# Moving full-precision transposes and state products together on TensorE in a hybrid encoder block

## The chip, the cores and the metric

The kernel runs on one core of a Trainium2 chip, in one launch. The metric is the device time of an execution in microseconds, taken as the median of several runs. A profile of one execution (the profiled execution) gives the trace: which engine ran which instruction when. The engines are TensorE (PE: matrix multiplies and transposes, results in PSUM), VectorE (DVE), ScalarE (ACT), GpSimd (POOL) and SyncE (SP, which issues most DMAs). Each engine works through its own queue in a fixed order; they meet through semaphores. "PE at" and "PE mm" in the profile's lines name the PSUM tile that is written (`at` or `mm`); they are no waits.

## The reference

One layer on x of 512 tokens by 1024 channels. Cut to what matters here:

```python
h = rms_norm(x, mix_norm_g)
proj = h @ w_in          # mLSTM q,k,v,o,gates | neighbourhood q,k,v | memory q | merge gates
y_ml = mlstm_branch(...) # 4 heads of 128, forward and backward, states per 64-token chunk
y_na = neighbourhood_attention(...)  # 8 heads of 64 on an 8 x 64 grid, 16 columns wide
y_xa = memory_cross_attention(...)   # 4 heads of 128 into 256 memory tokens
merged = g_ml*(y_ml @ w_br_ml) + g_na*(y_na @ w_br_na) + g_xa*(y_xa @ w_br_xa)
x = x + merged @ w_out
x = x + conv_glu_ffn(rms_norm(x), ...)   # d_ff = 2816
return rms_norm(x)
```

All of it is float32. The mLSTM branch weighs query-key products with exponentials of gate sums and adds what a running state (C) holds for the chunks before (or, backward, behind). Neighbourhood attention is softmax attention with a bias table, in windows.

## The kernel before

**Precision.** A large product is made of three fp32r matmuls: each operand is split into a high part (ScalarE copies it to fp32r) and a low part (VectorE subtracts), and `mm3` (lines 212 to 215) multiplies high by high, high by low and low by high. Small products and all transposes (against `ident`) run on TensorE in plain float32.

**Stream of weights.** The weights lie in DRAM as a list of blocks in the order of use. `weights(key)` (line 201) has SP load three blocks ahead (`wr`) and has ScalarE and VectorE split one block ahead (`wh` at line 195, `wl` at line 196). `proj(key, ...)` (line 395) then runs 24 matmuls of 512 columns (256 for the memory keys) into one PSUM tile of the pool `mmp` (four banks, tag `mm`). The small stages use the pool `atp` (four banks, tag `at`).

**Side work in steps.** The mixers are written as Python generators: `ml_all` (mLSTM), `xa_all` (memory attention), `na_all` (neighbourhood attention). They run one after another, and `step(n)` (line 1108) advances the current one by n `yield`s, with fractions kept in `quota`. The main code calls `step` inside and after its projections, so that each piece of a mixer stands between the matmuls of a projection. `drain` (line 1181) runs a mixer to its end before its branch product needs the result. Functions put on the list `late` are emitted by `flush` at certain places in `proj` and in `states`. The program text gives each instruction its rank; the order of each engine's queue is then worked out for the whole program before it runs, so an instruction may stand ahead of earlier text if its inputs are ready sooner. `tc.issue_after(ins)` keeps an instruction behind `ins` on the same engine.

**mLSTM, one head h, two steps.** `keys(h)` (line 679) transposes the head's keys with four turns (line 684), splits keys and queries, and puts on `late` the function `weigh`, which scales the values (lines 705, 709, 711). `states(h)` (line 718) multiplies keys by weighed values: four float32 products (line 729; each product is two instructions) and two `mm3` (line 732), then adds up the running states C (lines 741, 743) and splits them (line 747). `exps` makes the exponentials, `mask` adds the causal mask. `weights_J(h, o)` (line 757) does the half o of the head: two query-key products (line 765), `turn_J` for the half before (turns of the pair weights E, line 804), the edge chunk's product with C (line 769), and the *pair product* with the split states, one `mm3` of 258 columns (line 772); then VectorE forms the weights E (lines 776 to 791). `values_J` (line 808) multiplies the turned E by the values. In the loop (line 865) the first step of head h ends with `load_R(h + 1)` (two DMAs of the gate rows on SP) and `keys(h + 1)`, whose splits are kept behind `st["inter"]` and `st["mix"]`, the end of this step's pair product; the second step ends with `states(h + 1)`.

**Neighbourhood attention, 16 steps i (8 heads, two half grids).** `prep` splits queries and keys of a pair of heads, with the low parts of the queries in zero-padded tiles `QZ` (two pairs of tiles, line 906). `scores(i)` (line 934): four fp32r matmuls, then bias, exponential and normalisation on VectorE and ScalarE. `transposes(i)` (line 960): four turns (line 963) and their split into two tiles `w` (tag `E`, two buffers). `values(i)` (line 975): four fp32r matmuls (line 982). `store(i)`: lines 994 to 1003 write the split result into `yh`, `yl`. The loop (line 1011) does, in round t, scores(t), values(t - 2), transposes(t - 1). `load_vwin` has GpSimd issue 32 DMAs for the value windows of the next pair of heads, four rounds before they are needed. The rounds fall between the gate projections and branch products of the last two thirds of the merge.

Of the kernel before, what the change touches and what calls it, by code (L numbers as in the profile page):

```python
# [110 lines left out]
def hybrid_block(ctx, tc, xg, xT, memT, wflat, vecs, gbias, nabias, outa, outb, outc):  # L111
# [104 lines left out]

    def split_act(h, l, src, scale=1.0):

        A.activation(h, src, AF.Copy, scale=scale)  # L219
        V.scalar_tensor_tensor(l, src, scale, h.bitcast(F32), op0=ALU.mult, op1=ALU.subtract)  # L220


    vec = cp.tile([P, NVEC], F32, name="vec")
# [438 lines left out]
    def ml_all():  # L662
# [55 lines left out]
        def states(h, k, w, C, q, R, ee):  # L718

            flush()  # L720
            dec = ml["dec"]
            (ke, kh, kl), (ew, wh, wl) = k, w
            pc = [mmps() for _ in range(2)]
            po = (0, 130, 0, 131)
            at = lambda J, d: pc[J // 2][:, po[J] + 129 * d:po[J] + 129 * d + 129]
            for J in (0, 3, 1, 2):
                if J in (0, 3):
                    e = J // 3
                    PE.matmul(at(J, e), ke[:, e * P:(e + 1) * P], ew[e], start=True, stop=True)
                else:  # L730
                    o, js = po[J], slice((J - 1) * P, J * P)
                    mm3(pc[J // 2][:, o:o + 258], kh[:, js], kl[:, js], wh[J - 1], wl[J - 1], True, True)
            tj = [tp.tile([P, 2 * M], F32, tag="nab", name=nm("C")) for _ in range(2)]
            pair = lambda j, d: tj[j][:, 129 * d:129 * d + 129]
            one = [t[:, 258:387] for t in tj]
            C.extend([[pair(0, 0), pair(1, 0), one[0]], [one[1], pair(0, 1), pair(1, 1)]])
            for d in range(2):
                last = None
                for i in range(3) if d == 0 else range(2, -1, -1):
                    if last is None:  # L740
                        A.activation(C[d][i], at(i + d, d), AF.Copy)
                    else:
                        V.scalar_tensor_tensor(C[d][i], C[d][last], dec[:, d, i + d - 1, h:h + 1], at(i + d, d),
                                               op0=ALU.mult, op1=ALU.add)
                    last = i
            for j in range(2):
                split_act(wh[j], wl[j], tj[j][:, :258])

        def exps(h, o, R):

# [3 lines left out]
                    with tc.issue_after(st["act"]):  # L754
                        A.activation(w, w, AF.Exp, bias=ml["br"][:, d, J, h:h + 1])

        def weights_J(H, ss, h, o, k, w, C, q, R, ee):

            num = ml["num"]
            edge = 0 if o == 0 else NT - 1  # L760
            ps = {}
            for J in (o, o + 1):
                ps[J] = atps()
                hs = slice(h * S + J * P, h * S + (J + 1) * P)
                PE.matmul(ps[J][:, 384:], qT[:, hs], kT[:, hs], start=True, stop=True)  # L765
            turn_J()
            pi = {J: p[:, :258].rearrange("p (d c) -> p d c", d=2) for J, p in ps.items()}
            e, hs = 1 - edge // (NT - 1), slice(h * S + edge * P, h * S + (edge + 1) * P)
            PE.matmul(pi[edge][:, e], qT[:, hs], C[e][edge - 1 + e], start=True, stop=True)
            i = 1 if o == 0 else 2  # L770
            qs = slice((i - 1) * P, i * P)
            mm3(ps[i][:, :258], q[0][:, qs], q[1][:, qs], w[1][i - 1], w[2][i - 1], True, True)
            E = tp.tile([P, 4, P], F32, tag="E", name=nm("E"))
            y = tiny(12)
            init, den, r = [y[:, x:x + 4].rearrange("p (j d) -> p j d", j=2) for x in (0, 4, 8)]
            V.tensor_tensor(init[:, edge - o, e:e + 1], pi[edge][:, e, 128:129], num[:, e, edge, h:h + 1], op=ALU.mult)
            V.tensor_tensor(init[:, i - o], pi[i][:, :, 128], num[:, :, i, h], op=ALU.mult)
            for J in (o, o + 1):
                for d in range(2):
                    p = R[d][:, J * P:(J + 1) * P]  # L780
                    V.tensor_tensor_reduce(p, p, ps[J][:, 384:], 1.0,
                                           init[:, J - o, d:d + 1] if J == i or d == e else 0.0,
                                           ALU.mult, ALU.add, accum_out=den[:, J - o, d:d + 1])
            V.scalar_tensor_tensor(den, den, -1.0, den, op0=ALU.mult, op1=ALU.max)
            V.tensor_tensor(den, den, em.rearrange("p t (a b) -> p t a b", b=4)[:, o:o + 2, 0:9:8, h], op=ALU.max)
            V.reciprocal(den, den)
            for j in range(2):
                js = slice((o + j) * P, (o + j + 1) * P)
                V.tensor_scalar(E[:, j], R[0][:, js], den[:, j, 0:1], None, op0=ALU.mult)
                st["mix"] = V.scalar_tensor_tensor(E[:, j], R[1][:, js], den[:, j, 1:2], E[:, j], op0=ALU.mult,  # L790
                                                   op1=ALU.add).ins
            V.tensor_tensor(r, num[:, :, o:o + 2, h].rearrange("p d j -> p j d"), den, op=ALU.mult)
            Hj = lambda J: H[:, J * P:(J + 1) * P]
            A.activation(Hj(edge), pi[edge][:, e, 0:128], AF.Copy, scale=r[:, edge - o, e:e + 1])
            st["inter"] = A.activation(Hj(i), pi[i][:, 0, 0:128], AF.Copy, scale=r[:, i - o, 0:1]).ins
            V.scalar_tensor_tensor(Hj(i), pi[i][:, 1, 0:128], r[:, i - o, 1:2], Hj(i), op0=ALU.mult, op1=ALU.add)
            fresh.append((H, ss, h, o, E))
# [48 lines left out]
        last = prev = None  # L846
        open_J, turned, fresh = [], [], []

        def keyed(h, *ins):
            return keys(h, nxt, tp.tile([P, S], F32, tag="H", name=nm("ee"), bufs=4), *ins)  # L850

        def over():
            open_J.extend(fresh)
            fresh.clear()

        nxt = load_R(0)
        st_h = keyed(0)
        yield
        states(0, *st_h)
        ml["rows"]()  # L860
# [4 lines left out]
        for h in range(4):  # L865
            own, R = st_h, nxt
            values_J()
            if h > 1:
                flush()
                emit_y(h - 2, last[0])  # L870
            last = prev
            prev = tp.tile([P, S], F32, tag="H", name=nm("H"), bufs=4), tiny(4)
            weights_J(*prev, h, 0, *own)
            exps(h, 2, R)
            if h < 3:
                nxt = load_R(h + 1)
                st_h = keyed(h + 1, st["inter"], st["mix"])
                for d in range(2):
                    late.append(lambda d=d, n=nxt, i=st["mix"]: mask(n, d, i))
            over()  # L880
            yield
            values_J()
            scale = normalise(*last) if last else None
            weights_J(*prev, h, 2, *own)
            if scale:
                late.append(lambda f=scale, i=st["inter"]: f(i))
            over()
            if h < 3:
                states(h + 1, *st_h)
                exps(h + 1, 0, nxt)  # L890
            yield
        values_J()
# [10 lines left out]

    def na_all(nq, nk, vw0, yh, yl):

        QZ = [[tp.tile([P, S], F32R, tag="H", name=nm("QZ"), bufs=4) for _ in range(2)] for _ in range(2)]
        for pair in QZ:
            for e in range(2):
                G.memset(pair[e][64 - 64 * e:128 - 64 * e].bitcast(F32), 0.0)

        def prep(hp):
            qn = nq[:, hp * S:(hp + 1) * S]
            kn = nk[:, hp * S:(hp + 1) * S]
            QL = QZ[hp % 2]
            QS, KS = [], []
            for e in range(2):
                own, oth = slice(64 * e, 64 * e + 64), slice(64 - 64 * e, 128 - 64 * e)
# [42 lines left out]
        def transposes(i, sm):  # L960
# [3 lines left out]

            pp = []
            for bl in range(2):
                w = tp.tile([P, 4, P], F32R, tag="E", name=nm("w")).rearrange("p a b -> p (a b)")
                wv = w[:, :512].rearrange("p (k x q) -> p k x q", k=2, x=2)
                src = pt[:, bl * 256:(bl + 1) * 256].rearrange("p (k q) -> p k q", k=2)
                A.activation(wv[:, :, 0, :], src, AF.Copy)  # L970
                V.tensor_tensor(wv[:, :, 1, :], src, wv[:, :, 0, :].bitcast(F32), op=ALU.subtract)
                pp.append(w)
# [35 lines left out]
        sms, pts = {}, {}  # L1008
        vws = {0: vw0}
        yield  # L1010
        for t in range(n + 2):
            if t < n:
                nb = bias_tile(t + 1) if t + 1 < n else None
                sms[t] = scores(t, ops, bt)
                bt = nb
                if t % 4 == 3 and t + 1 < n:
                    ops = prep((t + 1) // 4)
            i = t - 2
            if 0 <= i:
                if i % 4 == 0 and i + 4 < n:  # L1020
                    vws[i // 4 + 1] = load_vwin(i // 4 + 1)
                store(i, values(i, pts.pop(i), vws[i // 4]))
            i = t - 1
            if 0 <= i < n:
                pts[i] = transposes(i, sms.pop(i))
            yield


# [525 lines left out]
```

## Time and profile before

| | |
|---|---|
| median of 3 runs | 873.08 us (872.96 to 873.76) |
| profiled execution | 873.18 us |
| its span, first to last instruction | 871.2 us |
| TensorE clock granted | 1.000 |
| DMA | 99.81 MB, mean 115 GB/s |

The busy share of an engine is the time in which an instruction of it was running. A line of a group gives the program line, engine, operation, written and read tiles, the count, the busy time, the mean duration in ns and the idle time before. Matmuls overlap: a 512-column matmul lasts 0.39 us in the profile, and the next one starts 0.23 us after it. In the chain that ended last, each piece is counted from the end of the piece before, so that lengths add up to the span. The profiled execution's time exceeds its span by 2.0 us.

### The profile page before, as it was taken

What the parts mean: (1) busy time and instruction counts of PE and PEld (TensorE: products, weight loads), DVE (VectorE), ACT (ScalarE), POOL (GpSimd) and SP (SyncE); (2) the same over time, 40 slices, a digit from 0 to 9 for tenths busy, and PEclk for the clock granted to TensorE, in tenths of its full rate; (3) what the DMA queues carried; (4) which work ended last, traced back from release to release, by engine and by line L of the source; (5) the groups of instructions that cost most, each with busy time, mean ns of one, the idle gap of its engine ahead of it and who ended that gap; (6) DMA issues with size and microseconds to landing.
All of it is one profiled execution on the core that took longest, in us unless ns stands there. A gap on an engine that the chain in (4) does not pass through costs nothing.

```text
span 871.2 us, 12230 instructions
## 1 busy us (share of the span) xinstructions
PE 865.8 (99%) x4287; PEld 733.9 (84%) x4287; DVE 594.7 (68%) x1292; ACT 467.8 (54%) x981; POOL 125.4 (14%) x202
## 2 busy tenths in 40 slices
PE   9999999999999999999999999999999999999997
PEld 7898889888888888888888888888888888888887
DVE  7794698997477768897676558776633466666534
ACT  7563577764355658897534455444422344444532
POOL 0101100000344370600000002111100011111010
PEclk9999999999999999999999999999999999999999
DMA  8324643533343453533223433323233323232412
GB/s 281 101 75 147 196 140 89 169 107 115 93 132 82 113 146 112 160 116 122 99 96 109 144 109 97 98 96 98 78 98 113 102 96 97 96 98 87 141 35 97
DMA packets 39421, 99.81 MB, mean 115 GB/s; under 512 B 5688, under 2 KB 13880, under 8 KB 39360
## 3 DMA queue, kind: packets, MB, share of 16 engines
q1 hardware_dynamic: 31568, 92.32, 32.6%
q0 software_dynamic: 7360, 6.32, 3.4%
q8 instruction: 34, 0.56, 0.3%
q10 hardware_dynamic: 432, 0.39, 0.1%
q14 instruction: 27, 0.22, 0.1%
HBM read 94.80 MB, written 4.21 MB: 114 GB/s over the span
## 4 chain that ended last, share of the span: by engine, by line
PE 98%; DVE 1%; issue 0%; ACT 0%; POOL 0%; POOLq 0%
PE mm L213 29%; PE mm L215 29%; PE mm L214 29%; PE at L214 2%; PE at L213 2%; PE at L215 2%; PE at L982 1%; PE at L963 1%; PE at L944 0%; PE at L945 0%; PE at L765 0%; PE at L813 0%; PE at L1070 0%; PE at L243 0%; PE mm L422 0%
## 5 line engine op out<-in xcount | busy, mean ns | idle before, releaser
L213 PE MATMUL mm<-u,wh 128*128 128x512 f32 (+1 forms) x1072 | 414.3, 386 | 0.0
L215 PE MATMUL mm<-u,wl 128*128 128x512 f32 (+1 forms) x1072 | 411.8, 384 | 0.0
L214 PE MATMUL mm<-u,wh 128*128 128x512 f32 (+1 forms) x1072 | 411.5, 384 | 0.0
L195 ACT ACTIVATE wh<-wr 128x512 fp32r<-128x512 f32 (+2 forms) x298 | 184.2, 621 | 219.9 <-PE mm L214 177.2
L196 DVE TENSOR_TENSOR wl<-wr,wh 128x512 fp32r<-128x512 f32 (+3 forms) x300 | 203.4, 681 | 88.5 <-ACT wh L195 86.4
L215 PEld LDWEIGHTS mm<-u,wl 128*128 128x128 f32 x1072 | 201.3, 188 | 40.3 <-DVE wl L196 0.4
L213 PEld LDWEIGHTS mm<-u,wh 128*128 128x128 f32 x1072 | 201.5, 188 | 39.0 <-ACT wh L195 0.4
L214 PEld LDWEIGHTS mm<-u,wh 128*128 128x128 f32 x1072 | 201.5, 188 | 38.5
L1418 POOL TENSOR_TENSOR s<-s,rb 128x512 f32<-128x512 f32 x22 | 38.2, 1736 | 401.7 <-DVE s L1417 238.9
L540 POOL DMA_DIRECT2D u<-nav_d x128 | 62.5, 535 | 70.5 <-DVE X L220 24.3
L219 ACT ACTIVATE u<-s 128x512 fp32r<-128x512 f32 x26 | 16.4, 632 | 56.4 <-DVE s L1421 56.3
L1421 DVE TENSOR_TENSOR s<-mm,s 128x512 f32<-128x512 f32 x22 | 15.2, 690 | 23.9 <-POOL s L1418 23.9
L460 ACT ACTIVATE s<-pad,vec 128x512 f32<-128x512 f32 x30 | 24.4, 813 | 9.7 <-DVE pad L458 9.7
L220 DVE SCALAR_TENSOR_TENSOR u<-s,u 128x512 fp32r<-128x512 f32 x26 | 19.1, 733 | 14.8 <-ACT u L219 14.5
L461 DVE SCALAR_TENSOR_TENSOR s<-pad,vec,s 128x512 f32<-128x512 f32 x30 | 22.5, 750 | 5.5 <-ACT s L460 5.5
L1417 DVE SCALAR_TENSOR_TENSOR s<-s,s 128x512 f32<-128x512 f32 x22 | 15.2, 691 | 13.4 <-ACT s L1416 13.3
L462 DVE SCALAR_TENSOR_TENSOR s<-pad,vec,s 128x512 f32<-128x512 f32 x30 | 22.5, 750 | 0.9
L1416 ACT ACTIVATE s<-s 128x512 f32<-128x512 f32 x22 | 13.9, 632 | 14.9 <-DVE s L1415 14.9
L1196 DVE TENSOR_TENSOR s<-mm,rb_x 128x512 f32<-128x512 f32 x16 | 11.0, 689 | 13.8 <-PE mm L215 13.7
L458 DVE TENSOR_TENSOR pad<-mm,rb 128x512 f32<-128x512 f32 x22 | 15.1, 690 | 6.4 <-PE mm L215 6.2
L1428 DVE TENSOR_TENSOR u<-mm,u 128x512 f32<-128x512 f32 x13 | 9.0, 692 | 14.6 <-PE mm L215 14.6
L214 PE MATMUL mm<-wl,u 128*128 128x512 f32 x48 | 18.7, 390 | 0.0
(352 smaller groups left out, 1053.3 us busy)
## 6 DMA issues: line engine op xcount, KB each, us to landing
wr<-wflat SPq DMA_DIRECT2D x141, 512.0 KB, 3.3
nab<-nabias SPq DMA_DIRECT2D x16, 256.0 KB, 2.7
u<-nav_d POOLq DMA_DIRECT2D x128, 32.0 KB, 2.8
s<-xT SPq DMA_DIRECT2D x15, 256.0 KB, 4.0
wr<-wflat SPq DMA_DIRECT2D x14, 192.0 KB, 2.4
nav_d<-nv POOLq DMA_DIRECT2D x8, 256.0 KB, 2.5
R<-rd SPq DMA_DIRECT2D x8, 256.0 KB, 4.6
wr<-wflat SPq DMA_DIRECT2D x2, 544.0 KB, 3.4
```

Of the source, the lines that this page charges most:

```text
L195: A.activation(h[:, u:v], src, AF.Copy)
L196: V.tensor_tensor(l[:, u:v], src, h[:, u:v].bitcast(F32), op=ALU.subtract)
L213: PE.matmul(ps, lh, rh, start=start, stop=False)
L214: PE.matmul(ps, lh, rl, start=False, stop=False)
L215: st["mm"] = PE.matmul(ps, ll, rh, start=False, stop=stop).ins
L219: A.activation(h, src, AF.Copy, scale=scale)
L220: V.scalar_tensor_tensor(l, src, scale, h.bitcast(F32), op0=ALU.mult, op1=ALU.subtract)
L460: A.activation(t1, pad[:, 0:512], AF.Identity, scale=vcol(w, i), bias=vcol(b, i))
L461: V.scalar_tensor_tensor(t1, pad[:, 1:513], vcol(w, n + i), t1, op0=ALU.mult, op1=ALU.add)
L462: V.scalar_tensor_tensor(t1, pad[:, 2:514], vcol(w, 2 * n + i), t1, op0=ALU.mult, op1=ALU.add)
L540: G.dma_start(vw[r * 32:(r + 1) * 32, i * 256:(i + 1) * 256], nav_v[hf, r, CW[b]:CW[b] + 32, hp * 256:(hp + 1) * 256])
L1418: G.tensor_tensor(c, c, rb2, op=ALU.mult)
```

## The change

Four things, with the work itself unchanged:

- `weights_J` takes a function `mid` and calls it right after the edge product (line 769), ahead of the pair product. In a head's first step `mid` issues `load_R(h + 1)` and `keys(h + 1)`; in the second step `states(h + 1)`.
- The splits in `keys(h + 1)` are kept behind the last split of `states(h)` (`st["parts"]`) and no longer behind the end of this step's pair product. The masks of the next head stay behind the pair product.
- Neighbourhood attention: in every even round t the turns of steps t - 2 and t - 1 are issued together, between the values and the scores. Values come first in a round and belong to step t - 3. There are 19 rounds in place of 18.
- The split weights of odd steps get two tiles of their own (`odd`, tag `H`); to make room, `QZ` keeps one pair of tiles (`QL`) in place of two.

```diff
     def split_act(h, l, src, scale=1.0):
-        A.activation(h, src, AF.Copy, scale=scale)
-        V.scalar_tensor_tensor(l, src, scale, h.bitcast(F32), op0=ALU.mult, op1=ALU.subtract)
+        a = A.activation(h, src, AF.Copy, scale=scale).ins
+        return a, V.scalar_tensor_tensor(l, src, scale, h.bitcast(F32), op0=ALU.mult, op1=ALU.subtract).ins
...
             for j in range(2):
-                split_act(wh[j], wl[j], tj[j][:, :258])
+                st["parts"] = split_act(wh[j], wl[j], tj[j][:, :258])
...
-        def weights_J(H, ss, h, o, k, w, C, q, R, ee):
+        def weights_J(mid, H, ss, h, o, k, w, C, q, R, ee):
...
             PE.matmul(pi[edge][:, e], qT[:, hs], C[e][edge - 1 + e], start=True, stop=True)
+            mid()
             i = 1 if o == 0 else 2
...
-            weights_J(*prev, h, 0, *own)
+            ahead = []
+
+            def next_keys():
+                if h < 3:
+                    R = load_R(h + 1)
+                    ahead.extend((R, keyed(h + 1, R, *st["parts"])))
+
+            weights_J(next_keys, *prev, h, 0, *own)
             exps(h, 2, R)
             if h < 3:
-                nxt = load_R(h + 1)
-                st_h = keyed(h + 1, st["inter"], st["mix"])
+                nxt, st_h = ahead
...
-            weights_J(*prev, h, 2, *own)
+
+            def next_states():
+                if h < 3:
+                    states(h + 1, *st_h)
+
+            weights_J(next_states, *prev, h, 2, *own)
             if scale:
                 late.append(lambda f=scale, i=st["inter"]: f(i))
             over()
             if h < 3:
-                states(h + 1, *st_h)
                 exps(h + 1, 0, nxt)
...
-        QZ = [[tp.tile([P, S], F32R, tag="H", name=nm("QZ"), bufs=4) for _ in range(2)] for _ in range(2)]
-        for pair in QZ:
-            for e in range(2):
-                G.memset(pair[e][64 - 64 * e:128 - 64 * e].bitcast(F32), 0.0)
+        QL, odd = [[tp.tile([P, S], F32R, tag="H", name=nm(n), bufs=4) for _ in range(2)] for n in ("QZ", "w")]
+        for e in range(2):
+            G.memset(QL[e][64 - 64 * e:128 - 64 * e].bitcast(F32), 0.0)
...
-                w = tp.tile([P, 4, P], F32R, tag="E", name=nm("w")).rearrange("p a b -> p (a b)")
+                if i % 2:
+                    w = odd[bl]
+                else:
+                    w = tp.tile([P, 4, P], F32R, tag="E", name=nm("w")).rearrange("p a b -> p (a b)")
...
-        for t in range(n + 2):
+        for t in range(n + 3):
+            i = t - 3
+            if 0 <= i:
+                if i % 4 == 0 and i + 4 < n:
+                    vws[i // 4 + 1] = load_vwin(i // 4 + 1)
+                store(i, values(i, pts.pop(i), vws[i // 4]))
+            if t % 2 == 0 and 2 <= t <= n:
+                for i in (t - 2, t - 1):
+                    pts[i] = transposes(i, sms.pop(i))
             if t < n:
...
-            i = t - 2
-            if 0 <= i:
-                if i % 4 == 0 and i + 4 < n:
-                    vws[i // 4 + 1] = load_vwin(i // 4 + 1)
-                store(i, values(i, pts.pop(i), vws[i // 4]))
-            i = t - 1
-            if 0 <= i < n:
-                pts[i] = transposes(i, sms.pop(i))
             yield
```

More of the change, by code (lines that the diff above doesn't have):

```diff
@@ L847, in ml_all, with keyed @@
         open_J, turned, fresh = [], [], []
-        def keyed(h, *ins):
-            return keys(h, nxt, tp.tile([P, S], F32, tag="H", name=nm("ee"), bufs=4), *ins)
+        def keyed(h, R, *ins):
+            return keys(h, R, tp.tile([P, S], F32, tag="H", name=nm("ee"), bufs=4), *ins)
         def over():
@@ L856, in ml_all @@
         nxt = load_R(0)
-        st_h = keyed(0)
+        st_h = keyed(0, nxt)
         yield
@@ L913, in prep @@
             kn = nk[:, hp * S:(hp + 1) * S]
-            QL = QZ[hp % 2]
             QS, KS = [], []
```

## The prediction

> **What bounds the kernel now.** I read the page from the top: span, busy time, the chain that ended last. Then I asked what TensorE (PE) waits for, and last I looked at single stretches of its queue.
>
> ```profile
> span 871.2 us, 12230 instructions
> ...
> PE 865.8 (99%) x4287; PEld 733.9 (84%) x4287; DVE 594.7 (68%) x1292; ACT 467.8 (54%) x981; POOL 125.4 (14%) x202
> ...
> DVE  7794698997477768897676558776633466666534
> ...
> PE 98%; DVE 1%; issue 0%; ACT 0%; POOL 0%; POOLq 0%
> ```
>
> TensorE is busy for 865.8 of 871.2 us and 98% of the chain is its own matmuls. "Busy" could still hide stalls, because the ends of matmuls are modelled; so I asked for its waits:
>
> ```profile
> PE at L243 <- PEq L1541: 0.8, 1, 0.8
> ```
>
> That is the whole list, and it lies in the warm-up at the start. In the two stages that the change touches (mLSTM, roughly 116 to 232 us, and neighbourhood attention, 312 to 430 us) nothing holds TensorE up. So a gain can come only from matmuls that themselves get cheaper, and a loss from any wait that is new. The digits of DVE (one per 21.8 us) say where a wait would come from: in the mLSTM stage VectorE is at 8 and 9 tenths.
>
> **The change part by part.** No matmul, transpose, copy or split is added or removed; on GpSimd two memsets of `QZ` go, on an engine at 14%. What changes is the order. Full-precision work (transposes against `ident`, and the products at L729, L765, L769, L813) stands between split-precision (fp32r) matmuls, and the change brings neighbouring groups of it together:
>
> ```profile
> L963 PE MATMUL at<-ident,s 128*128 128x128 f32 x64 | 9.6, 272 | 0.0
> ...
> L684 PE MATMUL mm<-ident,u 128*128 128x128 f32 x16 | 2.6, 272 | 0.0
> ...
> L729 PE MATMUL mm<-ee,s 128*128 128x129 f32 x8 | 1.5, 275 | 0.0
> L729 PE MATMUL mm<-s 128*128 128x129 f32 x8 | 1.5, 272 | 0.0
> ```
>
> Attention: 64 turns in 16 groups of four become 8 groups of eight, so 8 groups fewer. mLSTM: the four key turns of heads 1 to 3 (L684) and the four state products of heads 1 to 3 (L729) move up beside L769, ahead of the pair product's three 258-column matmuls (L772): 3 + 3 groups fewer. That is 14 groups, and the question is what the end of one group costs. First the chain, where a piece's length is the time it takes from the stream:
>
> ```profile
> 249.91 0.87 PE at L1070 x8
> ...
> 325.60 0.44 PE at L963 x4
> ```
>
> Eight turns in one group (memory attention) take 0.87 us, four take 0.44: 0.109 and 0.110 each. A group has no visible entry or exit fee. The timeline shows starts, and it looks different at first:
>
> ```profile
> 324.97 0.63 PE L982 MATMUL at<-w,u 128*128 128x256 f32 x4
> 325.44 0.60 PE L963 MATMUL at<-ident,s 128*128 128x128 f32 x4
> 325.79 0.48 PE L213 MATMUL mm<-u,wh 128*128 128x512 f32 x1
> 326.11 0.39 PE L214 MATMUL mm<-u,wh 128*128 128x512 f32 x1
> ...
> 327.95 0.39 PE L213 MATMUL mm<-u,wh 128*128 128x512 f32 x1
> ...
> 331.35 0.28 PE L944 MATMUL at<-KS,QS 128*128 128x256 f32 x1
> ```
>
> From 327.95 to 331.35 run 15 matmuls of 512 columns: 3.40 / 15 = 0.227 us each. The first one after the turns (325.79) takes 0.32 to the next start, 0.09 too long. But the last turn is followed after only 0.03 instead of 0.11, so that matmul merely starts early: 0.08 of the 0.09 is the last turn's own time. The whole stretch settles it: 325.44 to 327.95 is 2.51 us for four turns and nine matmuls; 9 x 0.2267 + 4 x 0.109 = 2.476. The rest is **0.034 us per group**, mostly in the handful of matmuls after it. That is the most that one removed group can give: 14 x 0.034 = 0.48 us. Is it the turns that cost it? Here is a short run without any:
>
> ```profile
> 426.98 0.64 PE L982 MATMUL at<-w,u 128*128 128x256 f32 x4
> 427.45 0.40 PE L213 MATMUL mm<-u,wh 128*128 128x512 f32 x1
> ...
> 428.84 0.39 PE L213 MATMUL mm<-u,wh 128*128 128x512 f32 x1
> ```
>
> The six matmuls from 427.45 take 1.39 us where 6 x 0.2267 = 1.36 are due: 0.03 again, with no transpose near. So the fee belongs to a run of short matmuls, and in attention each step keeps such a run (four scores and four values), turns or not. There I take the difference between the chain's two rows, 0.44 - 0.87 / 2 = 0.005: 8 x 0.005 = 0.04 us. In mLSTM a run of short matmuls that stood apart, or was twice as broken up, does become one; there I take the whole 0.034: 6 x 0.034 = 0.20. Sum: **0.24 us**, bounds 0 (no run of short matmuls disappears) and 0.48.
>
> On the fee of a change the Trainium skill has a harder rule. "TensorEngine Tiling (Array Packing)", section Key Properties, says that changing the tiling mode drains TensorE. It speaks of tiling, not of precision, and all of these matmuls use 128 x 128. If a change of precision counted as such a change, the sum would be the rival "drain" below; the 0.109 and 0.110 per turn speak against it.
>
> What the moved steps carry along: `keys` starts with `load_R`, two DMAs on SP, now issued a few matmuls earlier.
>
> ```profile
> R<-rd SPq DMA_DIRECT2D x8, 256.0 KB, 4.6
> ```
>
> They refill the tiles of the head before, which the last products of that head release (L790, rows below: done at 147.29, where the next step's matmuls run at 149.7). If SP waits there, the weight loads behind it wait as well, but those are issued three blocks ahead, so I cost it at nothing; without that cover it would be up to their 4.6 us. On GpSimd the window loads (`load_vwin`) move one step later together with the values that need them; the lead of four steps stays. Attention as a whole ends one step later, see the rivals. Evacuating the turns of two steps at once puts two more copies of some 0.4 us on ScalarE and VectorE into even steps and takes them out of odd ones; the second step's copies land in tiles of their own and have a whole step more until they are read, so nothing waits behind them.
>
> **Sum.** The profiled execution took 873.18 us (span 871.2 and 2.0 around it). 873.18 - 0.24 = 872.94; the median of the runs, 873.08, lies 0.1 below the profiled one, so **872.9 us**. A measurement of this kernel can tell about 0.2% (1.75 us, 871.3 to 874.8) from no change, and this lies well within it.
>
> **The rivals.**
> *Late splits (slower).* The place is the memory-key stretch, where blocks are only 256 columns wide and VectorE is full:
>
> ```profile
> 140.20:149.20 9.00, 9.00 (x72) 8.73 (x71) 8.81 (x37) 8.59 (x26) 0.00 (x0) 1.00 0.20 72
> ```
>
> The columns after the span are PE, PEld, DVE, ACT, POOL: VectorE works 8.81 of 9.00 us. What hangs on it:
>
> ```profile
> 146.68 0.61 DVE L790 SCALAR_TENSOR_TENSOR E<-R,y,E 128x128 f32<-128x128 f32 x2
> ...
> 149.38 0.68 DVE L196 TENSOR_TENSOR wl<-wr,wh 128x512 fp32r<-128x512 f32 x1
> ...
> 153.95 0.42 DVE L693 TENSOR_TENSOR u<-mm,u 128x256 fp32r<-128x256 f32 x1
> ```
>
> ```profile
> 149.68 0.38 PE L804 MATMUL at<-ident,E 128*128 128x128 f32 x2
> ...
> 150.53 0.36 PE L215 MATMUL mm<-u,wl 128*128 128x256 f32 x1
> ```
>
> The low half of the weights is ready at 150.06, and TensorE uses it at 150.53: 0.47 us to spare. The pair weights `E` are ready at 147.29 for the turn at 149.68: 2.4 us. The changed `keys` no longer queues its VectorE work behind the pair product (`st["mix"]`) but behind a split of the step before, so it may come ahead of such splits:
>
> ```profile
> 180.13 0.28 DVE L705 TENSOR_SCALAR s<-u,wt 128x129 f32<-128x129 f32 x1
> 180.33 0.27 DVE L705 TENSOR_SCALAR ee<-u,wt 128x129 f32<-128x129 f32 x1
> ...
> 181.39 0.41 DVE L698 TENSOR_TENSOR u<-u,u 128x256 fp32r<-128x256 f32 x1
> 181.72 1.13 DVE L711 SCALAR_TENSOR_TENSOR u<-u,wt,u 128x129 fp32r<-128x129 f32 x4
> ```
>
> With L693 that is 0.42 + 0.28 + 0.27 + 0.41 + 1.13 = 2.51 us. From 0.47 us on TensorE stands still; all of it ahead gives 2.04 us, so 872.9 + 2.0 = **874.9**, and more if it happens at two heads. Against it: the work is not new, VectorE's total up to 150 us is the same, and the trace shows a static order that already lets next-block matmuls run between the pieces of a step. Less than all of it ahead ends between 873 and 874.9.
> *Nothing moves.* The order of issue is worked out for the whole program by which inputs are ready when, so a group written together can be split again:
>
> ```profile
> 150.49 0.28 PE L684 MATMUL mm<-ident,u 128*128 128x128 f32 x1
> ...
> 153.00 0.49 PE L684 MATMUL mm<-ident,u 128*128 128x128 f32 x3
> ```
>
> One head's key turns stand 2.5 us apart here. If the groups stay apart the time is 873.1.
> *The pause counts in full.* If the 0.09 us after each group were lost and not borrowed from the last turn, 14 x 0.09 = 1.3 us would go: 871.8. The chain's two rows speak against it.
> *Drain.* If TensorE emptied at each change, a matmul's length beyond its step, 0.39 - 0.23 = 0.16 us, would be lost on entry and on exit: 28 x 0.16 = 4.5 us less, 868.6. The step from L982 to L963 (0.47 for four, then four turns in 0.44) shows no such gap.
> *Late end of attention.* The last values move behind one more gate: its 24 matmuls of 0.227 us, 5.45, and the 0.47 of the values before them, 5.92 us later.
>
> ```profile
> 429.76 0.49 DVE L1003 TENSOR_TENSOR u<-s,u 64x128 fp32r<-64x128 f32 x2 [0.37 <-ACT u L1002]
> ...
> 438.56 0.69 DVE L1196 TENSOR_TENSOR u<-mm,rb_x 128x512 f32<-128x512 f32 x1 [1.54 <-PE mm L215]
> ```
>
> Now the last store ends 3.27 us after the values begin (426.98 to 430.25); shifted, it ends at 436.2, and the branch that reads it begins when the last gate is done, 438.56. That leaves 2.4 us. Were the chain to take twice as long, 0.9 us would be lost: 873.8.
>
> **How the numbers follow.** Forecast (872.9, 872.4 to 873.4) 0.67; late splits 0.17; nothing moves 0.06; the pause in full 0.05; drain 0.03; late end 0.02. Faster by over 0.2% is drain alone: 0.03. Slower by over 0.2% is late splits, all of which I put there although its mild end lies inside: 0.17. Within 0.2% is the rest, 0.80. The range goes from 872.2 (forecast with the upper bound of the gain and the spread of the runs) to 875.2 (late splits at their price); the pause and drain are left out below, and a double stall above.
>
> **What would show it.** Right: TensorE's list of waits stays as it is; L963 appears in groups of eight lasting 0.87 in the chain, L684 and L729 directly behind L769; the stretch after a group still carries about 0.03 us; busy times of VectorE and ScalarE are unchanged. Wrong on the fee: fewer groups and a span more than 0.5 us shorter, with 512-column steps still at 0.227. Wrong on the cover: steps of TensorE over 0.25 us between 140 and 180 us, with a low half (L196) or an `E` (L790) ending just before the late matmul; or a gap after 438 us behind L1003.

## The result, and the profile after

The changed kernel takes **875.51 us** (median of 9 runs, 874.97 to 875.9) against 873.02 us before (9 runs in turn with it, 872.8 to 873.76): 1.0026 times as long, 95% interval 1.0017 to 1.0035. The forecast was 872.9, the range 872.2 to 875.2. The profiled execution took 875.38 us. Its page, the lines that answer to those of before (span, busy time, VectorE's digits, shares of the chain that ended last):

```profile
span 873.5 us, 12236 instructions
...
PE 867.1 (99%) x4287; PEld 734.2 (84%) x4287; DVE 594.6 (68%) x1292; ACT 468.3 (54%) x981; POOL 124.0 (14%) x200
...
DVE  7794798987477668888676658776633466666534
...
PE 91%; ACT 4%; DVE 4%; issue 1%; POOL 0%; POOLq 0%; DVEq 0%
```

VectorE and ScalarE are as busy as before. What is new is the last line: 8% of the chain is now ScalarE and VectorE, where it was 1%. TensorE's list of waits has one line more than the one of the warm-up:

```profile
PE at L972 <- ACT s L966: 0.9, 2, 0.6
```

L972 are the turns of neighbourhood attention (L963 before), L966 is the last step of the softmax, which writes what they turn. To find where the 2.3 us of span arise I cut it at three instructions that both kernels have: the first small product of the mLSTM branch (L628), the first scores (L944, now L953), and VectorE's read of the last gate before the branch product (L1196, now L1208). The timeline of before, and then of after:

```profile
117.83 0.53 PE L628 MATMUL at<-lfc,ident 128*128 128x32 f32 x4
...
312.16 0.28 PE L944 MATMUL at<-KS,QS 128*128 128x256 f32 x1
```

```profile
117.78 0.53 PE L628 MATMUL at<-lfc,ident 128*128 128x32 f32 x4
...
312.53 0.28 PE L953 MATMUL at<-KS,QS 128*128 128x256 f32 x1
...
440.88 0.69 DVE L1208 TENSOR_TENSOR u<-mm,rb_x 128x512 f32<-128x512 f32 x1 [1.54 <-PE mm L215]
```

With 438.56 for L1196 (quoted in the prediction) the **mLSTM stretch** grew from 194.33 to 194.75 us and the **attention stretch** from 126.41 to 128.35 (unrounded starts; the rows can differ by 0.01). What follows is the same: 871.2 - 438.56 = 432.6 and 873.5 - 440.88 = 432.6. So +0.42 us in mLSTM, +1.94 in attention.

In attention it can be read turn by turn. The timeline of after, TensorE, rounds t = 8, 10, 12 and 14:

```profile
365.51 0.60 PE L972 MATMUL at<-ident,s 128*128 128x128 f32 x4
366.42 0.84 PE L972 MATMUL at<-ident,s 128*128 128x128 f32 x4 [0.31 <-ACT s L966]
367.01 0.37 PE L953 MATMUL at<-KS,QS 128*128 128x256 f32 x1
...
379.95 1.44 PE L972 MATMUL at<-ident,s 128*128 128x128 f32 x8
381.14 0.36 PE L953 MATMUL at<-KS,QS 128*128 128x256 f32 x1
...
394.04 0.60 PE L972 MATMUL at<-ident,s 128*128 128x128 f32 x4
395.22 0.84 PE L972 MATMUL at<-ident,s 128*128 128x128 f32 x4 [0.58 <-ACT s L966]
395.81 0.37 PE L953 MATMUL at<-KS,QS 128*128 128x256 f32 x1
...
408.71 1.03 PE L972 MATMUL at<-ident,s 128*128 128x128 f32 x8
409.50 0.37 PE L953 MATMUL at<-KS,QS 128*128 128x256 f32 x1
```

From the first turn to the first score behind the eight: 0.79 us in round 14, as it should be, but 1.50, 1.19 and 1.77 in rounds 8, 10 and 12. That is 0.71 + 0.40 + 0.98 = 2.09 us lost, each time in the second four, the odd step's turns. The stretch grew by 0.15 less than this; a gain of that size, with this order of the rounds, is measured by itself below.

The list of waits shows 0.9 of these 2.09 us. A wait there counts from the end of the matmul before, and that end is modelled; the distance of starts shows all of it. The Trainium skill says so too ("Perfetto Trace Analysis", section Tensor Engine Instruction (MATMUL, LD_WEIGHTS)): TensorE's end times are estimated. The 2.09 us by the starts and the 0.9 by the list fit that. The list of TensorE's weight loads (PEld) is nearer: each turn is preceded by a load, and these loads wait for the softmax in all three groups, twice in each (366.42 and 366.82, 380.55 and 380.95, 395.21 and 395.61):

```profile
PEld at L972 <- ACT s L966: 2.2, 6, 0.8
```

**Why the odd step is late.** One round's softmax in after: TensorE, VectorE and ScalarE from the scores of step 11 (round 11) to the turns in round 12.

```profile
387.63 0.28 PE L953 MATMUL at<-KS,QS 128*128 128x256 f32 x1
...
389.78 0.41 DVE L1007 TENSOR_TENSOR s<-s,at 64x256 f32<-64x256 f32 x1
...
390.72 0.41 DVE L1008 TENSOR_TENSOR s<-s,at 64x256 f32<-64x256 f32 x1
391.05 0.41 DVE L958 CUSTOM_DVE_ANT_0 s<-at,nab 128x256 f32<-128x256 f32 x1
...
393.03 0.69 DVE L932 TENSOR_TENSOR KS<-u,KS 64x512 fp32r<-64x512 f32 x1
393.74 0.69 DVE L933 TENSOR_TENSOR QZ<-u,QS 64x512 fp32r<-64x512 f32 x1
393.95 0.19 ACT L963 ACTIVATION_READ_ACCUMULATOR s<-s,y 128x1 f32 x1
394.45 0.17 DVE L964 RECIPROCAL y<-y 128x2 f32<-128x2 f32 x1
394.65 0.91 ACT L966 ACTIVATE s<-s,y 128x256 f32<-128x256 f32 x2 [0.52 <-DVE y L964]
```

And the same step before:

```profile
386.28 0.28 PE L944 MATMUL at<-KS,QS 128*128 128x256 f32 x1
...
387.09 0.42 DVE L949 CUSTOM_DVE_ANT_0 s<-at,nab 128x256 f32<-128x256 f32 x1
...
391.08 0.89 ACT L957 ACTIVATE s<-s,y 128x256 f32<-128x256 f32 x2
...
394.11 0.60 PE L963 MATMUL at<-ident,s 128*128 128x128 f32 x4
```

Before, VectorE adds the bias (L949) 0.81 us after the scores begin, the softmax ends at 391.97, 5.7 us after they begin, and the turns are due at 394.11: 2.1 us to spare. After, the bias (L958) begins 3.4 us after the scores, behind the store (L1007, L1008), which the round now issues ahead of the scores; the reciprocal (L964) stands behind two splits of `prep`, though its sum was there at 394.14. The softmax ends at 395.56, 7.9 us after the scores begin. And the turns are due sooner: the odd step's four at 394.04 + 4 x 0.11 = 394.48, 6.85 us after the scores, where before it was 7.83. So 2.2 us later on one side and 1.0 sooner on the other, against 2.1 to spare.

The Trainium skill says in the same section that the queues of VectorE and ScalarE are strictly first in, first out. The reciprocal that is ready at 394.14 and starts at 394.45 agrees.

### The profile page after: what moved, and what is told of

The parts are those of the page before. It is cut to its first block, busy times and chain, and to the rows that moved or that the text cites. A ratio compares the mean times of both kernels' runs of the same rounds, so it can differ in the third digit from the quotient of the medians.

```text
span 873.5 us, 12236 instructions
## 1 busy us (share of the span) xinstructions
PE 867.1 (99%) x4287; PEld 734.2 (84%) x4287; DVE 594.6 (68%) x1292; ACT 468.3 (54%) x981; POOL 124.0 (14%) x200
## 4 chain that ended last, share of the span: by engine, by line
PE 91%; ACT 4%; DVE 4%; issue 1%; POOL 0%; POOLq 0%; DVEq 0%
PE mm L213 27%; PE mm L215 27%; PE mm L214 27%; PE at L214 2%; PE at L213 2%; PE at L215 2%; DVE w L983 1%; ACT s L966 1%; ACT wh L195 1%; ACT s L963 1%; DVE wl L196 1%; PE at L765 0%; PE at L814 0%; PE at L1082 0%; PE at L972 0%
## 5 line engine op out<-in xcount | busy, mean ns | idle before, releaser
L963 ACT ACTIVATE s<-s,y 128x256 f32<-128x256 f32 x32 | 16.0, 502 | 10.6 <-DVE y L960 10.6
L1208 DVE TENSOR_TENSOR s<-mm,rb_x 128x512 f32<-128x512 f32 x16 | 11.0, 689 | 14.9 <-PE mm L215 14.9
```

The lines of the kernel that those rows point to most:

```text
L963: A.activation(smv[:, j, :], smv[:, j, :], AF.Exp, bias=mx[:, j:j + 1], accum_out=su[:, j:j + 1])
```

## The experiments

All medians in one table; "before" ran in turn with each group of kernels. Stretches are from each kernel's profile, cut as above. From the last cut to the end it is 432.6 us in all of them, and the start-up ahead of L628 lies between 117.67 and 118.50 us in these kernels, none of which touches it; so effects below half a microsecond are read from the stretches, not from span or median.

| kernel | median us | before us | ratio, 95% interval | mLSTM us | attention us |
|---|---|---|---|---|---|
| before | | | | 194.33 | 126.41 |
| the change | 875.51 | 873.02 | 1.0026, 1.0017 to 1.0035 | 194.75 | 128.35 |
| mLSTM half (ml_only) | 873.96 | 873.30 | 1.0007, 0.9998 to 1.0016 | (195.07) | 126.47 |
| attention half (na_only) | 875.08 | 873.30 | 1.0021, 1.0012 to 1.0029 | 194.34 | 128.31 |
| change, store behind the scores (store_last) | 873.45 | 873.30 | 1.0002, 0.9993 to 1.0011 | 194.74 | 126.27 |
| change, turns last in the round (turns_last) | 873.85 | 873.30 | 1.0005, 0.9996 to 1.0014 | 194.75 | 126.41 |
| attention, turns behind values and scores (values_first) | 874.03 | 873.42 | 1.0007, 0.9998 to 1.0017 | 194.34 | 127.11 |
| tiles alone (tiles_only) | 873.21 | 873.42 | 0.9997, 0.9987 to 1.0006 | 194.33 | 126.41 |
| attention of store_last alone (best_na) | 873.16 | 873.31 | 0.9997, 0.9988 to 1.0006 | 194.34 | 126.26 |
| keys early (keys_only) | 874.29 | 873.31 | 1.0010, 1.0001 to 1.0019 | 195.22 | 126.41 |
| states early (states_only) | 874.25 | 873.31 | 1.0010, 1.0001 to 1.0019 | 195.40 | 126.41 |
| states early, other banks (states_at) | 873.45 | 873.42 | 1.0001, 0.9992 to 1.0010 | 194.53 | 126.41 |
| key turns early, splits late, states early (keys_behind_na) | 874.40 | 873.31 | 1.0011, 1.0002 to 1.0020 | 195.52 | 126.28 |
| key turns early alone (turns_only_na) | 873.19 | 873.42 | 0.9999, 0.9990 to 1.0008 | 194.31 | 126.27 |

(The profile of ml_only was granted a clock of 0.949, so its stretch is not compared, only its median.)

My theory after the result: the odd step's softmax is late in attention because the round issues store and `prep` ahead of it and turns right behind the values; a smaller loss comes from mLSTM, apart from that. Rivals: the tiles (one pair of `QL`, own tiles for odd steps) make something wait; or the place of the turns alone decides, whatever the store's rank; or most of the loss is VectorE in mLSTM, as the forecast's "late splits" had it.

**Each half alone.** `ml_only` keeps the attention part of before, `na_only` the mLSTM part.

> Only the mLSTM half of the change; neighbourhood attention as before. Theory: most of the 2.4 us comes from attention, where the turns of the odd step now wait for that step's softmax; the mLSTM half costs 0.4 us (waits at 140.5 and 173 us). Then 873.4 us, no wait of TensorE in attention. Rival, that the mLSTM half (splits of the next head's keys ahead of the pair weights E, as the prediction's slow case had it) is the main cause: 875 us.

> Only the attention half; mLSTM as before. Theory: 875.0 us, with waits of TensorE of together some 2 us at the turns of steps 7, 9 and 11. Rival, mLSTM is the cause: 873.0 us.

The attention half alone has 1.90 of the 1.94 us (128.31 us). The mLSTM half adds some 0.7 us to the median, where 0.4 had been expected, with an interval that reaches no change. That "late splits" is most of the loss, is out.

**The order inside the rounds.** `store_last` is the whole change with the store and `prep` moved behind the scores:

```diff
-                store(i, values(i, pts.pop(i), vws[i // 4]))
+                k, py = i, values(i, pts.pop(i), vws[i // 4])
...
                 bt = nb
-                if t % 4 == 3 and t + 1 < n:
-                    ops = prep((t + 1) // 4)
+            if t >= 3:
+                store(k, py)
+            if t % 4 == 3 and t + 1 < n:
+                ops = prep((t + 1) // 4)
```

`turns_last` is the whole change with scores (and `prep`) first in a round, then values and store, then the pair of turns.

> The whole change, but in each round the store of the values and the splitting of the next heads' queries and keys are written after the scores, so that the softmax ranks ahead of them on VectorE and ScalarE; TensorE's order is written as in the change. Theory (softmax of the odd step is queued behind the store): the waits at the odd turns shrink from 2.1 us to under 0.7, 873.5 to 874.2 us. Rival (two steps' evacuations at once are too many, or the tiles): unchanged, 875.4.

> The whole change, but each round keeps the order of before: scores, values, then in even rounds the turns of two steps. Pairs, own tiles for odd steps and one pair of low query tiles stay. Theory (turns and softmax too close): no wait of TensorE in attention, 873.3 us (the mLSTM half's 0.4 left, 0.1 gained by the pairs). Rival burst (eight copies at once) or rival tiles: 875 us.

Neither loses against before in attention (126.27 and 126.41). The timeline of store_last, the round of the rows above:

```profile
386.66 0.28 PE L953 MATMUL at<-KS,QS 128*128 128x256 f32 x1
...
389.31 0.42 DVE L958 CUSTOM_DVE_ANT_0 s<-at,nab 128x256 f32<-128x256 f32 x1
...
390.19 0.41 DVE L1007 TENSOR_TENSOR s<-s,at 64x256 f32<-64x256 f32 x1
...
392.80 0.91 ACT L966 ACTIVATE s<-s,y 128x256 f32<-128x256 f32 x2 [0.27 <-DVE y L964]
...
393.07 1.13 PE L972 MATMUL at<-ident,s 128*128 128x128 f32 x8
393.95 0.36 PE L953 MATMUL at<-KS,QS 128*128 128x256 f32 x1
```

The bias comes ahead of the store, 2.7 us after the scores in place of 3.4; the softmax ends at 393.71, 7.05 us after them in place of 7.9; the eight turns take 0.88 us, 0.09 over the 0.79, so here the softmax is only just in time. The new place of store and `prep` thus takes back 0.85 of the 2.2 us. The softmax still ends 1.35 us later than the 5.7 of before, and what makes that part is not shown; without the 0.85 it is no longer late enough to cost much. Which share of this is the store's rank and which `prep`'s was not tried apart; that the waits were longest in rounds 8 and 12, the ones behind a round with `prep` (7 and 11), speaks for both.

**A dose.** If lateness is a matter of amounts, turns that stand half a microsecond later should lose half a microsecond less. `values_first` keeps the store ahead of the scores as in the change (mLSTM as before), and moves only the pair of turns behind the four scores (0.48 us):

```diff
                 store(i, values(i, pts.pop(i), vws[i // 4]))
-            if t % 2 == 0 and 2 <= t <= n:
-                for i in (t - 2, t - 1):
-                    pts[i] = transposes(i, sms.pop(i))
             if t < n:
...
                     ops = prep((t + 1) // 4)
+            if t % 2 == 0 and 2 <= t <= n:
+                for i in (t - 2, t - 1):
+                    pts[i] = transposes(i, sms.pop(i))
```

> Attention half alone (mLSTM as before). A round is now: values and store of the step three back, then scores, then the turns of two steps at the end of even rounds. The store keeps its rank ahead of the scores' softmax, as in the change; only the turns stand four score products (about 0.48 us) later than with the attention half as made. Theory (late softmax of the odd step, a matter of amounts): the three waits of 0.71, 0.41 and 0.99 us shrink by about 0.5 each, to some 0.75 us or less in all, and the attention stretch (126.41 us before, 128.31 with the half as made) becomes 126.8 to 127.3 us. Rival (the place of the turns right behind the values decides alone): 126.4 us and no wait. Rival (the store's rank decides alone): 128.3 us.

The stretch is 127.11 us, where amounts gave 126.8 to 127.3 and the rivals 126.4 and 128.3. The timeline, rounds 10 and 12:

```profile
380.08 1.04 PE L961 MATMUL at<-ident,s 128*128 128x128 f32 x8
380.87 0.48 PE L213 MATMUL mm<-u,wh 128*128 128x512 f32 x1
...
393.79 0.60 PE L961 MATMUL at<-ident,s 128*128 128x128 f32 x4
394.76 0.84 PE L961 MATMUL at<-ident,s 128*128 128x128 f32 x4 [0.36 <-ACT s L955]
```

Round 10 is in time (0.79 us), as is round 8, where 0.2 us were expected to stay; round 12 still waits, 394.76 in place of 393.79 + 0.44, because there the softmax itself ends later, 8.2 us after its scores (395.11 and 386.90) in place of 7.9. So the theory holds in its sum, not in each term.

**The tiles.** `tiles_only` makes before's rounds run with one pair `QL` and the two `odd` tiles.

> Rounds and mLSTM as before; only the tiles change: one pair of low-part tiles QL in place of two, and the odd steps' weights in two tiles of their own. Theory (the order inside the rounds makes the loss, not the tiles): attention stretch 126.41 us as before, no wait of TensorE, 873.1 us. Rival (one pair QL makes the next pair's queries wait for the last scores): over 127 us and a wait of TensorE at the scores.

126.41 us and no wait: the tiles cost nothing.

**What the grouping gives.** `best_na` is the attention part of store_last with before's mLSTM: the pairs of turns, without late softmax.

> mLSTM as before; attention with pairs of turns, and the store and the preparation written after the scores. The mLSTM stretch (first product of L628 to the first scores) should be 194.33 us as before, the attention stretch (first scores to the last gate's read) 126.27 as in the run with the store last, against 126.41 before. Theory: 0.15 us faster than before, 872.9 to 873.1, no wait. Rival (the gain of the pairs was noise): 873.2.

The stretch is 126.26, **0.15 us** shorter than before. But best_na differs from before in the order inside a round as well (values, turns, scores). turns_last has the same eight groups of eight in the order of before (scores, values, turns), and gains nothing: 126.41. Two steady rounds, from scores to scores, take 13.73 us before (338.22 to 351.95), 13.73 in turns_last (338.31 to 352.04) and 13.68 in best_na (338.42 to 352.10). So eight groups fewer give nothing by themselves; the gain comes with the order that puts the scores, in place of the turns, ahead of the 512-column matmuls. Whether this order would give it without the pairs was not tried. The whole kernel is not distinguishable from before by its time (0.9988 to 1.0006).

**The mLSTM part.** It costs 0.42 us in the changed kernel. `keys_only` moves `load_R` and `keys` up, and leaves the states where they were; `states_only` does the reverse, with the keys' splits behind the pair product as before.

```diff
-            weights_J(next_states, *prev, h, 2, *own)
+            weights_J(lambda: None, *prev, h, 2, *own)
...
             over()
             if h < 3:
+                next_states()
```

```diff
-            weights_J(next_keys, *prev, h, 0, *own)
+            weights_J(lambda: None, *prev, h, 0, *own)
             exps(h, 2, R)
             if h < 3:
+                st["parts"] = st["inter"], st["mix"]
+                next_keys()
```

> Only the key turns (with their splits and the two loads) ahead of the pair product; states where they were, attention as before. Theory: the 0.42 us that the mLSTM stretch lost is E coming late, because the next head's splits go ahead of it: the stretch is 194.6 to 194.8 us with a late L805 at 140 us. Rival (the states, whose additions go ahead of E): 194.33.

> Only the states ahead of the pair product; keys where they were, behind the pair product, attention as before. Theory: the mLSTM stretch is 194.3 to 194.45 us. Rival (states cause the loss): 194.6 to 194.8.

Alone they cost 0.89 and 1.07 us, more than both together and more than either expectation allowed (194.8 at most). The halves don't add up: the queues are worked out anew for each program, and each has another wait. In keys_only it is the wait of the whole change, and a second one of the same kind 19 us later: the turns of a pair's weights E are late. The timeline of before, and then of after, around head 1 (ScalarE, VectorE, TensorE):

```profile
129.67 1.28 ACT L337 ACT_TABLE_LOAD   x1
...
139.69 0.37 ACT L794 ACTIVATE H<-at,y 128x128 f32<-128x128 f32 x1 [0.24 <-DVE y L792]
...
138.98 0.60 DVE L790 SCALAR_TENSOR_TENSOR E<-R,y,E 128x128 f32<-128x128 f32 x2
...
140.21 0.60 PE L765 MATMUL at<-u,u 128*128 128x128 f32 x4
140.65 0.38 PE L804 MATMUL at<-ident,E 128*128 128x128 f32 x2
```

```profile
128.57 1.27 ACT L709 ACTIVATE u<-u,wt 128x129 fp32r<-128x129 f32 x4
...
130.38 1.28 ACT L337 ACT_TABLE_LOAD   x1
...
140.38 0.37 ACT L795 ACTIVATE H<-at,y 128x128 f32<-128x128 f32 x1 [0.96 <-DVE y L793]
...
139.66 0.61 DVE L791 SCALAR_TENSOR_TENSOR E<-R,y,E 128x128 f32<-128x128 f32 x2
...
140.15 0.60 PE L765 MATMUL at<-u,u 128*128 128x128 f32 x4
140.80 0.44 PE L805 MATMUL at<-ident,E 128*128 128x128 f32 x2
```

The weighed values of the next head (L709) now run ahead of the gate's table load, which begins 0.71 us later, and VectorE, which waits for that gate, ends E 0.69 later (140.27 for 139.58). E is still in time: its turns follow the four products that begin at 140.15, and before they did so after 0.44 us, which would be 140.59. But ScalarE's read L795 waits for a small tile `y` that VectorE makes behind E (L793); it ends at 140.75, where the same read (L794) ended at 140.06 before. The turns start 0.05 us after it, 0.65 us behind the first of the four products in place of 0.44. The only tile that this read and the turns share is a bank of `at`, which the one reads and the others write, and the list of weight loads names the same read (0.2 us at L805). In keys_only's second wait it is plainer: E had ended at 158.90 when its turns began at 160.17, and the list puts 0.3 us down to VectorE's read L797, which ended at 160.02. The 0.21 us at 140 are half of the 0.42; most of the rest lies at 174 us, where turns are late in small steps. So it is the forecast's rival "late splits" after all, in a mild form, some nine microseconds earlier than it was placed, through ScalarE and a PSUM bank that is read late. In states_only the wait is another one, TensorE and VectorE:

```profile
162.82 0.39 PE L729 MATMUL mm<-s 128*128 128x129 f32 x2
...
163.73 0.41 DVE L1164 TENSOR_TENSOR u<-mm,rb_m 128x256 f32<-128x256 f32 x1
...
164.19 0.49 PE L729 MATMUL mm<-ee,s 128*128 128x129 f32 x2 [0.87 <-DVE u L1164]
```

The second state product (a head has two, of two instructions each) writes to a bank of the pool `mm` that VectorE still has to read: L1164 takes a block of memory keys out of it at 163.73, and TensorE starts 0.05 us after that read ends. In `states_at` the states' products use the other pool:

```diff
-            pc = [mmps() for _ in range(2)]
+            pc = [atps() for _ in range(2)]
```

> The states half of the mLSTM edit alone, as in the run with only the states moved, but the states' products are written to banks of the other PSUM pool (at). Theory (the states' product waited 0.87 us for a bank of the pool mm, held by the read of a memory-key tile that VectorE reached late): that wait at 163 us is gone and the mLSTM stretch falls from 195.40 to about 194.4 us. Rival (VectorE is late with all that it feeds, whatever the bank): about 195.4 us, with a wait at another product in the same place.

The wait at 163 is gone and the stretch is 194.53 us. But this is not a clean proof: with the other pool the order changed as well, the products that stood at 162.82 and 164.19 now stand at 165.32 and 172.11. The 0.2 us that the stretch keeps over before's lie at 172: its start comes 0.29 us after the matmul before it in place of 0.23, its two take 0.25 in place of the 0.14 at 165.32. What is shown is the wait for VectorE's read of that bank, 0.87 of the 1.07 us; the bank, the order around it and the products' being early are not separated.

Last, the key turns without what hangs on them. In `keys_behind_na` the four turns move up, the splits stay behind the pair product, the states move up; in `turns_only_na` the states stay as well. Both have best_na's attention.

```diff
-        def keys(h, R, ee, act=None, dve=None):
+        def turn_keys(h):
...
+            return pt
+
+        def keys(h, R, pt, ee, act=None, dve=None):
...
-                    ahead.extend((R, keyed(h + 1, R, *st["parts"])))
+                    ahead.extend((R, turn_keys(h + 1)))
...
-                nxt, st_h = ahead
+                nxt, pt = ahead
+                st_h = keyed(h + 1, nxt, pt, st["inter"], st["mix"])
```

> Key turns and states ahead of the pair product, but the splits of the keys and queries and the weighing of the values written after the pair product and kept behind its end, as before; attention with the store last. Theory: the late E at 140 us goes, the mLSTM stretch is 194.2 to 194.4 us, attention 126.27; 872.8 to 873.1. Rival (the turns' and products' place is what costs): 194.7 and 873.4.

> mLSTM: only the four key turns move up beside the edge product; the keys' splits stay behind the pair product, the states stay where they were. Attention as changed, but with the store ranked behind the scores (126.27 us). Theory (VectorE's and PSUM's order, not the turns, costs in mLSTM): mLSTM stretch at most 194.4 us, 872.9 to 873.1 us in all. Rival (a PSUM bank taken early holds up something else): 194.7 to 195.5 us, with a wait of TensorE between 140 and 190 us.

keys_behind_na removes the wait at head 1, which bears out that the early splits made it, and gets the late bank of states_only (a wait of 1.0 us at the same read): 195.52, where 194.2 to 194.4 had been expected. turns_only_na has neither: 194.31 us, and 873.19 in all, not to be told from before. So the three groups of key turns give 0.02 us, which is no more than equal work differs by from program to program. No version beats the kernel before by more than a measurement can tell.

## Why the prediction was wrong, step by step

**What bounds the kernel: right.** A loss could come only from new waits of TensorE, and what was traced of it did: 2.09 us in attention, less 0.15, and half or more of the 0.42 in mLSTM.

**The fee of a group: small, as forecast, but miscounted in mLSTM.** The forecast gain was 0.04 us in attention and 0.20 in mLSTM. Measured in attention: 0.00 for the pairs in the order of before, 0.15 with the scores behind them. For the key turns it is 0.02 in place of 3 x 0.034 = 0.10. That term took six runs of short matmuls to disappear, and the trace of before shows that most of them were none of their own: key turns and state products already stood right behind the pair product's last 258-column matmul.

```profile
174.94 0.29 PE L215 MATMUL at<-u 128*128 128x258 f32 x1
175.07 0.60 PE L684 MATMUL mm<-ident,u 128*128 128x128 f32 x4
```

So it is for the key turns at 131.58 us and the state products at 141.45, 162.98 and 185.39, which the same matmul precedes by 0.12 us each; of the six, only the key turns split between 150.49 and 153.00 stood apart. By the forecast's own reading, that the fee belongs to a run of short matmuls, the term was one fee and not six. The state products were never seen free of a wait; at one head they are not even together after the change (159.89 and 164.13 in after). The last step of the sum has a slip too: 872.94 less 0.1 is 872.8. Nothing hung on either.

**"So nothing waits behind them": the step that failed.** I looked at what reads the turned weights and found a whole step more. I did not look at what the turns read. Both rows were there: before, the turns of a step stood 7.83 us behind its scores, and its softmax took 5.7. The new order of a round brings an odd step's turns 1.0 us nearer to its scores, which alone takes 1.0 of the 2.1 us between the end of the softmax and the turns; and it moves the store ahead of the scores in the program text, so ahead of the softmax in VectorE's queue. That the text sets the ranks stands in the section on the kernel; I used it only for mLSTM. In place of nothing, this cost 2.09 us. VectorE's digits, which I quoted, have 8, 8 and 9 in slices 16 to 18 (327 to 392 us), where two of the three waits came and right behind which the third did; I read 8 and 9 in the mLSTM stage and stopped there.

**Late splits: a true rival with a wrong place and price.** It cost 0.42 us, not 2.04, half of it at head 1 before the memory keys. It came neither by the low half of the weights, whose 0.47 us I had measured, nor by E, which I had put down as safe by 2.4 us at another spot, but by a bank of PSUM that VectorE's lateness kept occupied, a cover that I had not examined.

**Hidden steps: right.** `load_R` early and the end of attention made no wait. The last store in after (L1015) ends at 438.01, 2.9 us ahead of the last gate's read at 440.88; 2.4 had been worked out.

**Drain and the pause in full: out.** Grouping eight pairs gave at most 0.15 us; sixteen changes of precision fewer at 0.16 us each would have given 2.6 in attention alone, and eight pauses of 0.09 us 0.7.

**The chances.** 0.80 on "within 0.2%" rested on the one cover that I had examined. The range ended at 875.2 because its worst case was mLSTM's; a second place that could wait would have moved its end, and the time lies 0.3 us above it.

## What to carry to other kernels

When an instruction is moved, write down two margins from the trace of before: how long until its result is read, and how long its inputs have been ready. The second is what was lost here, and the move changes it at both ends, since whatever is issued ahead of the producer on VectorE and ScalarE delays it as well. Where only the order is to change, put the new batch as late as its readers allow, and issue work that nobody waits for (stores, preparation of the next pair) behind the chain that the batch reads.

## What the runs showed of the hardware

- What short matmuls cost depended on their order and not on the number of groups. Eight pairs of turns with scores behind them gain 0.15 us over sixteen groups (126.26 and 126.41); the same pairs with 512-column matmuls behind them gain nothing (126.41).
- The list of TensorE's waits gave 0.9 us where the starts show 2.09, and left out round 10 (0.40 us) altogether: two entries, three late groups. The list of its weight loads had all three, with 2.2 us.
- Parts of one edit didn't add up: 0.89 and 1.07 us alone, 0.42 together, each with other waits in its trace.
- Equal work from program to program repeats to some 0.02 us per stretch (mLSTM 194.33, 194.33, 194.34 and 194.34 where it was untouched), while the start-up ahead of 118 us wanders by 0.8 us (117.67 to 118.50): stretches between two instructions tell apart what spans can't.
